# Block 3, recurrent branch: the small products of transitions and outputs grouped by shape, by turns in both column halves

## The chip, the cores and the metric

The kernel runs on one core of one Trainium2 chip. The metric is the device time of one execution in microseconds (us), as the median of several runs. A profile of one execution gives each engine's instructions: PE is the matrix engine's products, PEld its weight loads, DVE the vector engine, ACT the scalar engine, POOL the general one, SP the one that issues most transfers.

## The reference, cut to what matters

The reference chains three transformer blocks over 512 tokens of width 1024. The third block has two mixers side by side: a sparse attention and a recurrence with eight heads of width 64. The recurrence is a scan over the tokens:

```python
def wkv7_scan(r, w, k, v, a, b):
    def step(state, inp):
        r_t, w_t, k_t, v_t, a_t, b_t = inp
        sa = jnp.einsum('bhvk,bhk->bhv', state, a_t)
        state = state * w_t[:, :, None, :] + sa[..., None] * b_t[:, :, None, :] + v_t[..., None] * k_t[:, :, None, :]
        return state, jnp.einsum('bhvk,bhk->bhv', state, r_t)
    ...
    _, ys = lax.scan(step, jnp.zeros((B, H, N, N), jnp.float32), xs)

def rwkv7_mixer(...):
    ...
    y = wkv7_scan(rh, decay.reshape(B, T, H, N), kh, vh, -kk, kk * ah)
    mean = jnp.mean(y, axis=-1, keepdims=True)
    var = jnp.mean(jnp.square(y - mean), axis=-1, keepdims=True)
    y = ((y - mean) * lax.rsqrt(var + GN_EPS)).reshape(B, T, RWKV_WIDTH) * lnx_w + lnx_b
    ...
```

So per token each head's 64 x 64 state is multiplied by a matrix, a rank-one term is added, and the output is the new state times a vector, normalized per head. The mixers' outputs go through a projection and a feed-forward stage.

## The kernel before, in words

The scan is rewritten in 8 chunks of 64 tokens (`CH`, `NCH`), two chunks to a block of 128 tokens. In the function `rwkv_state` the whole is turned into matrix products. Tokens of a chunk or a head's 64 features lie on 64 of the 128 partitions: `half[0]` is partitions 0 to 63, `half[1]` the others. A product `mm(out, w, x)` contracts over the partitions of `w` and `x`; the columns of `w` become the partitions of `out`. So a `w` on 64 partitions uses one half of PE's rows, and an `out` on 64 partitions one half of its columns. The trace writes the shape as rows*columns: 64*64 or 128*64. All operands of these products are fp32, and the trace records each product as two weight loads and two matmuls.

Four small functions do the recurrence:

- `transition(n)` (L2470) makes, for chunk n, the matrix that carries the state over the chunk (`pg`, then added into `GT[:, n]` by DVE) and the chunk's own contribution (`ph`, copied to `S3[:, n]` by ACT). For each of the eight heads it has one product of the shape 64*64 (L2476, not for chunk 0) and one of the shape 128*64 (L2477). Head h writes the column half h % 2.
- `advance(n)` (L2482) multiplies the state into the next one: eight products of the shape 64*64 (L2486), and DVE adds.
- `queries(c)` (L2490) folds a correction into the queries `Rt`: 16 products of the shape 64*64 (L2496) per pair of heads.
- `outputs(tb)` (L2500) makes the outputs of one block of 128 tokens in two halves of four heads (s = 0, 1). For each head and each of the two chunks (e = 0, 1) one product of the shape 64*64 with the state (L2510, not for chunk 0) and one of the shape 128*64 with the chunk's own values (L2511) are added up in PSUM. Chunk e writes column half e. DVE then takes mean and variance per head (L2516, L2517), a reciprocal root (L104 to L108), and normalizes (L2520, L2521).

PSUM tiles come from `k.pst`: four buffers of the tag "g" and two each of "a" and "t". All of `pg`, `ph` and `p` here are "g".

The order of work is set in two places. The code emits in an order of its own: the loop at the end of `rwkv_state` runs transition, advance, queries and outputs with a `yield` after each, and `weave` (L368) runs one step of the attention at each `yield`. An attention step (L2004 on) has four stages of units that lie one step apart: scores on PE (L2093) with maximum on DVE (L2096) and exponential on ACT (L2098), transposes (L2107) with copies (L2108), values (L2117), and the closing of a group (L2120 to L2132). When the recurrence is through, the rest of the attention runs alone. Then a planner in the kernel's framework lays down the order on each engine: it mostly follows the emitted order, but puts an instruction ahead of another whose data or buffer isn't ready by its reckoning.

Of the kernel before, what the change touches and what calls it, by code (L numbers as in the profile page):

```python
# [13 lines left out]
OP = mybir.AluOpType  # L14
# [1712 lines left out]
CH = 64  # L1727
# [618 lines left out]
def rwkv_state(k, pool, dram, a, cst, r, yn):  # L2346

    nc = k.nc
    V, S, G = nc.vector, nc.scalar, nc.gpsimd
    mm = nc.tensor.matmul  # L2350
    BK, UV, GA, eC = r.BK, r.UV, r.GA, r.eC
    half = [slice(0, 64), slice(64, 128)]
    with ExitStack() as ctx:
        def t(shape, name, tag=None, bufs=1, dt=FT):
            return pool.tile(shape, dt, name=k.nm(name), tag=tag or name, bufs=bufs)
# [17 lines left out]
        for s in range(30, -1, -1):  # L2373
            n = 31 - s
# [20 lines left out]
        Rt = pool3.tile([P, 4, T], FT, name="Rt")  # L2395
# [25 lines left out]
        for x in range(32):  # L2421
            for e in range(2):
                mm(pw[x // 16][rows(e, 1), x % 16 * 32:x % 16 * 32 + 32], GAv[rows(e, 0), x, e, 32:64], N1T[rows(e, 0), x],
                   start=True, stop=True)
# [5 lines left out]
        for x in range(32):  # L2430
            for e in range(2):
                mm(pw[x // 16][rows(e, 0), x % 16 * 32:x % 16 * 32 + 32], W[rows(e, 1), x], Nv[rows(e, 1), x, 32:64],
                   start=True, stop=True)
# [10 lines left out]
        Xa = GX[:, 0].rearrange("p (m h d) -> p m h d", m=NT, d=64)  # L2444
        GT = GX[:, 1].rearrange("p (n c d) -> p n c d", n=NCH, d=64)
        G.tensor_tensor(GT, cst["i64"][:, None, None, :].to_broadcast([P, NCH, 4, 64]),
                        eC.rearrange("p c n -> p n c")[:, :, :, None].to_broadcast([P, NCH, 4, 64]), op=OP.mult)
        for m in range(NT):
            F = Fs[m]
            for h0 in (0, 4):  # L2450
# [10 lines left out]
        GR = [t([P, 2, NCH, CH], "GR0", tag="F0"), pool3.tile([P, 2, NCH, CH], FT, name="GR1", tag="F1"),  # L2461
              t([P, 2, NCH, CH], "GR2", tag="N1T"), pool3.tile([P, 2, NCH, CH], FT, name="GR3", tag="W")]
# [5 lines left out]
        S3 = r.zpool.tile([P, NCH, 4, 64], FT, name="S3", tag="zk")  # L2468

        def transition(n):  # L2470
            m, e = divmod(n, 2)
            pg, ph = k.pst("g", (P, 4, 64)), k.pst("g", (P, 4, 64))
            for h in range(8):
                o, hs = half[h % 2], slice(h * 64, (h + 1) * 64)
                if n:
                    mm(pg[o, h // 2], Xa[half[e], m, h], BK[half[e], n, hs], start=True, stop=True)  # L2476
                mm(ph[o, h // 2], BK[:, n, hs], UV[:, m, e, hs], start=True, stop=True)  # L2477
            S.activation(S3[:, n], ph, AF.Copy)
            if n:
                V.tensor_tensor(GT[:, n], GT[:, n], pg, op=OP.add)  # L2480

        def advance(n):  # L2482
            p = k.pst("g", (P, 4, 64))
# [16 lines left out]
        def outputs(tb):  # L2500
            yv = yn[:, tb].rearrange("p (h s d) -> p s h d", s=2, d=64)
            for s in range(2):
                o = slice(s * 64, (s + 1) * 64)
                p = k.pst("g", (P, 4, 64))
                for h in range(s, 8, 2):
                    for e in range(2):
                        n = tb * 2 + e
                        pq = p[half[e], h // 2]
                        if n:
                            mm(pq, Rt[o, h // 2, n * CH:(n + 1) * CH], S3[o, n - 1, h // 2], start=True, stop=False)  # L2510
                        mm(pq, GR[h // 2][:, h % 2, n], UV[:, tb, e, h * 64:(h + 1) * 64], start=n == 0, stop=True)  # L2511
                bs = t([P, 4, 6], "ybs", bufs=2)
                mv = t([P, 4, 2], "ymv", bufs=2)
                rs = t([P, 2, 4], "yrs", bufs=2)
                for h in range(4):
                    V.bn_stats(bs[:, h], p[:, h])  # L2516
                    V.bn_aggr(mv[:, h], bs[:, h])  # L2517
                V.tensor_scalar(rs[:, 0], mv[:, :, 1], 64e-5, None, op0=OP.add)
                k.rsqrt(pool, rs[:, 1], rs[:, 0], 4, [P, 4])
                V.tensor_tensor(yv[:, s], p, mv[:, :, 0:1].to_broadcast([P, 4, 64]), op=OP.subtract)  # L2520
                V.tensor_tensor(yv[:, s], yv[:, s], rs[:, 1][:, :, None].to_broadcast([P, 4, 64]), op=OP.mult)  # L2521

        transition(0)
        for n in range(1, NCH):
            transition(n)
            yield
            if n < NCH - 1:
                advance(n)
            yield
            if n <= 4:  # L2530
                queries(n - 1)
                yield
            if n >= 4:
                outputs(n - 4)
                yield
# [378 lines left out]
```

## Time and profile before

| | |
|---|---|
| median of 3 runs | 3262.9 us (3262.18 to 3266.67) |
| the profiled execution | 3260.15 us |
| its span, first to last instruction | 3258.4 us |
| mean granted clock of PE | 0.966 |
| instructions of the small products, 2702.6 to 2826 us: L2476, L2477 | 112, 128 |
| L2510, L2511 | 112, 128 |

In the rows of groups, the number behind the x is how many instructions there are, then their busy time in us and the mean of one in ns, then the idle time before them. In the rows of the timeline the first number is the start in us, the second the length of that piece; neighbouring pieces of PE overlap, since products are pipelined, so the price of one is read from start to start. In the windows the first columns are the stretch and its length, then each engine's busy time, and then the granted clock of PE as a share of full speed.

### The profile page before, as it was taken

What the parts mean: (1) busy time and instruction counts of PE and PEld (TensorE: products, weight loads), DVE (VectorE), ACT (ScalarE), POOL (GpSimd) and SP (SyncE); (2) the same over time, 40 slices, a digit from 0 to 9 for tenths busy, and PEclk for the clock granted to TensorE, in tenths of its full rate; (3) what the DMA queues carried; (4) which work ended last, traced back from release to release, by engine and by line L of the source; (5) the groups of instructions that cost most, each with busy time, mean ns of one, the idle gap of its engine ahead of it and who ended that gap; (6) DMA issues with size and microseconds to landing.
All of it is one profiled execution on the core that took longest, in us unless ns stands there. A gap on an engine that the chain in (4) does not pass through costs nothing.

```text
span 3258.4 us, 40500 instructions
## 1 busy us (share of the span) xinstructions
PE 3044.4 (93%) x16321; PEld 2319.7 (71%) x16321; DVE 1773.7 (54%) x3227; ACT 1033.1 (32%) x1608; POOL 282.8 (9%) x316
## 2 busy tenths in 40 slices
PE   9899997887787899999999999999999879999999
PEld 7777676443342788888777777888876767688887
DVE  3877755643432544345964656443477775564433
ACT  3666532110010422223323532322223245333221
POOL 0342010000000000001100320000023210000000
PEclk9999998999798999999999999999999989899999
DMA  4322125799899332333223244332333410123322
GB/s 145 97 75 82 62 71 227 317 421 421 354 421 407 108 104 88 107 104 121 94 84 97 87 159 149 104 104 91 104 99 103 137 47 21 66 74 104 100 87 84
DMA packets 240985, 466.38 MB, mean 143 GB/s; under 512 B 24722, under 2 KB 163380, under 8 KB 216732
## 3 DMA queue, kind: packets, MB, share of 16 engines
q1 hardware_dynamic: 230956, 431.95, 36.9%
q0 software_dynamic: 9840, 31.82, 2.9%
q8 instruction: 130, 2.13, 0.3%
q14 instruction: 59, 0.48, 0.0%
HBM read 441.17 MB, written 22.56 MB: 142 GB/s over the span
## 4 chain that ended last, share of the span: by engine, by line
PE 43%; DVE 6%; issue 1%; ACT 1%; POOL 0%; DMA 0%; DVEq 0%; ACTq 0%; POOLq 0%
PE pg L150 20%; PE pg L188 4%; PE pg L189 4%; PE pg L187 4%; DVE nprod L2376 1%; DVE wl L69 1%; PE pg L2117 1%; PE pt L2107 1%; PE pg L176 1%; PE pg L175 1%; PE pg L174 1%; PE pa L2093 1%; PE pt L1442 0%; PE pg L2511 0%; PE pg L2510 0%
## 5 line engine op out<-in xcount | busy, mean ns | idle before, releaser
L69 DVE TENSOR_TENSOR wl<-raw,wh 128x2048 fp32r<-128x2048 f32 (+3 forms) x211 | 438.4, 2078 | 455.9 <-ACT wh L68 455.8
L68 ACT ACTIVATE wh<-raw 128x2048 fp32r<-128x2048 f32 (+3 forms) x214 | 368.8, 1724 | 701.6 <-PE pg L150 344.4
L150 PE MATMUL pg<-x2h,wh 128*128 128x512 f32 (+2 forms) x1136 | 441.9, 389 | 0.0
L150 PE MATMUL pg<-x2h,wl 128*128 128x512 f32 (+2 forms) x1136 | 440.2, 388 | 0.0
L150 PE MATMUL pg<-x2l,wh 128*128 128x512 f32 (+2 forms) x1136 | 439.2, 387 | 0.0
L150 PEld LDWEIGHTS pg<-x2h,wl 128*128 128x128 f32 (+1 forms) x1136 | 212.8, 187 | 49.0 <-issue 7.3
L150 PEld LDWEIGHTS pg<-x2l,wh 128*128 128x128 f32 (+1 forms) x1136 | 212.8, 187 | 47.7 <-issue 6.4
L150 PEld LDWEIGHTS pg<-x2h,wh 128*128 128x128 f32 (+1 forms) x1136 | 212.9, 187 | 45.6 <-issue 3.0
L188 PE MATMUL pg<-wl,hh 128*128 128x512 f32 x608 | 238.5, 392 | 0.0
L189 PE MATMUL pg<-wh,hl 128*128 128x512 f32 x608 | 237.7, 391 | 0.0
L187 PE MATMUL pg<-wh,hh 128*128 128x512 f32 x608 | 236.5, 390 | 0.0
L1178 PE MATMUL pa<-w,mscr 128*32 128x512 f32 x1024 | 172.4, 675 | 51.7 <-DMA w<-w 49.5
L1178 PEld LDWEIGHTS pa<-w,mscr 128*32 128x32 f32 x1024 | 43.3, 122 | 156.8 <-issue 145.0
L188 PEld LDWEIGHTS pg<-wl,hh 128*128 128x128 f32 x608 | 114.2, 188 | 25.4 <-DVE wl L69 0.8
L187 PEld LDWEIGHTS pg<-wh,hh 128*128 128x128 f32 x608 | 114.1, 188 | 25.3
L189 PEld LDWEIGHTS pg<-wh,hl 128*128 128x128 f32 x608 | 114.2, 188 | 23.7
L187 PE MATMUL pg<-wh,x2h 128*128 128x512 f32 (+1 forms) x288 | 101.8, 354 | 2.2 <-ACT x2h L232 2.2
L189 PE MATMUL pg<-wh,x2l 128*128 128x512 f32 (+1 forms) x288 | 101.2, 351 | 0.0
L188 PE MATMUL pg<-wl,x2h 128*128 128x512 f32 (+1 forms) x288 | 100.8, 350 | 0.0
L150 PE MATMUL pg<-x1h,wh 128*128 128x512 f32 x224 | 89.8, 401 | 1.0 <-ACT po L2774 0.6
L150 PE MATMUL pg<-x1l,wh 128*128 128x512 f32 x224 | 89.3, 399 | 0.0
L150 PE MATMUL pg<-x1h,wl 128*128 128x512 f32 x224 | 89.1, 400 | 0.0
(897 smaller groups left out, 5924.6 us busy)
## 6 DMA issues: line engine op xcount, KB each, us to landing
w<-w SPq DMA_DIRECT2D x188, 1024.0 KB
raw<-w_in SPq DMA_DIRECT2D x45, 1024.0 KB
raw<-ffn_w_in SPq DMA_DIRECT2D x44, 1024.0 KB
raw<-w_ff SPq DMA_DIRECT2D x16, 1024.0 KB
raw<-w_ff SPq DMA_DIRECT2D x20, 768.0 KB
raw<-w_in SPq DMA_DIRECT2D x24, 512.0 KB
raw<-w_out SPq DMA_DIRECT2D x12, 1024.0 KB
raw<-ffn_w_out SPq DMA_DIRECT2D x16, 768.0 KB
```

Of the source, the lines that this page charges most:

```text
L68: nc.scalar.activation(h, t, AF.Copy)
L69: (nc.gpsimd if i in self.slow else nc.vector).tensor_tensor(l, t, f32v(h), op=OP.subtract)
L150: nc.tensor.matmul(p, w[:, c, s], x[:, c, t], start=first, stop=last)
L174: nc.tensor.matmul(p[:, t], wh[:, c, s], xh[:, c, t], start=c == 0, stop=False)
L175: nc.tensor.matmul(p[:, t], wh[:, c, s], xl[:, c, t], start=False, stop=False)
L176: nc.tensor.matmul(p[:, t], wl[:, c, s], xh[:, c, t], start=False, stop=c == nk - 1)
L187: nc.tensor.matmul(p, xh[:, c, t], wh[:, c, :ncol], start=start and c == 0, stop=False)
L188: nc.tensor.matmul(p, xh[:, c, t], wl[:, c, :ncol], start=False, stop=False)
L189: nc.tensor.matmul(p, xl[:, c, t], wh[:, c, :ncol], start=False, stop=stop and c == nk - 1)
L1178: nc.tensor.matmul(ph[s], xt[:, c, s], w[:, :, c], start=c == 0, stop=c == DC - 1)
L2093: mm(ps[s], qT[:, c + 4 * s, i * P:(i + 1) * P], kT[:, s, j, :W], start=j == 0, stop=j == 1)
L2107: nc.tensor.transpose(pt[:, j], prs[s][:, j * P:(j + 1) * P], k.ident)
```

## The change

In `transition` the eight products of the first shape come first, then DVE's add into `GT`, then the eight products of the second shape. In `outputs` the eight products of the shape 128*64 come first, by turns in both column halves, and then those of the shape 64*64, by turns as well (for block 0 only half 1 has any). The flag that starts an accumulation is now set once per tile and half, on head pair c = 0, and the later heads' first products find their part of the tile not yet written. The number of products, their operands and all else are the same.

```diff
             pg, ph = k.pst("g", (P, 4, 64)), k.pst("g", (P, 4, 64))
+            if n:
+                for h in range(8):
+                    mm(pg[half[h % 2], h // 2], Xa[half[e], m, h], BK[half[e], n, h * 64:(h + 1) * 64], start=True, stop=True)
+                V.tensor_tensor(GT[:, n], GT[:, n], pg, op=OP.add)
             for h in range(8):
-                o, hs = half[h % 2], slice(h * 64, (h + 1) * 64)
-                if n:
-                    mm(pg[o, h // 2], Xa[half[e], m, h], BK[half[e], n, hs], start=True, stop=True)
-                mm(ph[o, h // 2], BK[:, n, hs], UV[:, m, e, hs], start=True, stop=True)
+                hs = slice(h * 64, (h + 1) * 64)
+                mm(ph[half[h % 2], h // 2], BK[:, n, hs], UV[:, m, e, hs], start=True, stop=True)
             S.activation(S3[:, n], ph, AF.Copy)
-            if n:
-                V.tensor_tensor(GT[:, n], GT[:, n], pg, op=OP.add)
...
-                for h in range(s, 8, 2):
+                for c in range(4):
                     for e in range(2):
                         n = tb * 2 + e
-                        pq = p[half[e], h // 2]
+                        h = 2 * c + s
+                        mm(p[half[e], c], GR[c][:, s, n], UV[:, tb, e, h * 64:(h + 1) * 64], start=c == 0,
+                           stop=n == 0 and c == 3)
+                for c in range(4):
+                    for e in range(2):
+                        n = tb * 2 + e
                         if n:
-                            mm(pq, Rt[o, h // 2, n * CH:(n + 1) * CH], S3[o, n - 1, h // 2], start=True, stop=False)
-                        mm(pq, GR[h // 2][:, h % 2, n], UV[:, tb, e, h * 64:(h + 1) * 64], start=n == 0, stop=True)
+                            mm(p[half[e], c], Rt[o, c, n * CH:(n + 1) * CH], S3[o, n - 1, c], start=False, stop=c == 3)
```

## The prediction

> **What bounds the kernel now.** I read the page first: span, busy shares, and the chain of work that ended last.
>
> ```profile
> span 3258.4 us, 40500 instructions
> PE 3044.4 (93%) x16321; PEld 2319.7 (71%) x16321; DVE 1773.7 (54%) x3227; ACT 1033.1 (32%) x1608; POOL 282.8 (9%) x316
> PE 43%; DVE 6%; issue 1%; ACT 1%; POOL 0%; DMA 0%; DVEq 0%; ACTq 0%; POOLq 0%
> ```
>
> PE leads everywhere, but a share of the whole says nothing of one stage. So I looked up where the four lines of the edit run: L2476 and L2477 (transitions) and L2510 and L2511 (outputs). They lie between 2702.6 and 2826 us. The groups by line, then the windows, of that stretch and of the one ahead of it:
>
> ```profile
> L2511 PE MATMUL pg<-UV,GR 128*64 128x64 f32 x128 | 19.5, 254 | 0.0
> L2510 PE MATMUL pg<-S,Rt 64*64 64x64 f32 x112 | 18.9, 251 | 0.0
> L2477 PE MATMUL pg<-UV,BK 128*64 128x64 f32 x128 | 16.6, 253 | 0.0
> L2476 PE MATMUL pg<-BK,GX 64*64 64x64 f32 x112 | 15.8, 254 | 0.0
> ```
>
> ```profile
> 2702.60:2756.80 54.20, 54.00 (x534) 41.81 (x531) 25.41 (x86) 24.57 (x73) 3.84 (x3) 0.91 0.01 3
> 2756.80:2826.00 69.20, 68.80 (x524) 50.02 (x522) 32.09 (x202) 18.39 (x57) 2.53 (x2) 0.83 0.09 32
> 2680.60:2702.60 22.00, 22.00 (x212) 16.80 (x212) 12.66 (x43) 17.27 (x51) 1.28 (x1) 1.00 0.26 92
> ```
>
> The columns of the windows are PE, PEld, DVE, ACT and POOL busy, the granted clock, the DMA share and GB/s. PE is busy 122.8 of 123.4 us, DVE only 57.5, ACT 43.0, and DMA is nearly idle. Here PE time is kernel time, and the four lines hold some 71 us of busy time on it (records overlap, so the wall time is less; it is cut out below). An x of 128 is 64 products: each is recorded as two instructions.
>
> How PE spends that time shows in the timeline of the transition of chunk 1, which runs in the order of the code:
>
> ```profile
> 2703.25 0.33 PE L2476 MATMUL pg<-BK,GX 64*64 64x64 f32 x2
> 2703.50 0.33 PE L2477 MATMUL pg<-UV,BK 128*64 128x64 f32 x2
> 2703.76 0.32 PE L2476 MATMUL pg<-BK,GX 64*64 64x64 f32 x2
> ...
> 2707.36 0.44 PE L2093 MATMUL pa<-ksT,qT 128*128 128x128 f32 x2
> ```
>
> One product in the 64*64 shape, one in the 128*64 shape, and so on: 16 products from 2703.25 to 2707.36, 0.257 us each from start to start. The transition of chunk 5 has the same products, but there they did not alternate:
>
> ```profile
> 2762.68 0.68 PE L2476 MATMUL pg<-BK,GX 64*64 64x64 f32 x16
> 2763.29 0.85 PE L2093 MATMUL pa<-kwT,qT 128*128 128x256 f32 x4
> 2763.97 0.27 PE L2107 MATMUL pt<-ident,npr 128*128 128x128 f32 x1
> 2764.17 0.69 PE L2477 MATMUL pg<-UV,BK 128*64 128x64 f32 x16
> 2764.79 0.51 PE L2093 MATMUL pg<-kwT,qT 128*128 128x256 f32 x2
> ```
>
> Eight products of one shape, head by head and so by turns in both halves of the output columns, take 0.61 us (2762.68 to 2763.29), the eight others 0.62 (2764.17 to 2764.79): 0.077 us each. That is the order that the change writes for every transition, so its price stands in this trace.
>
> **The change part by part.** Removed: I cut the timeline into the stretches in which the two shapes alternate, and had their lengths added (first stretch and sum; transitions of chunks 1, 2, 3, 4 and 7 in seven pieces, then outputs of all four blocks in eleven):
>
> ```profile
> 2703.25:2707.36 4.11, 4.11 (x37) 1.00 0.02 4
> sum 23.43, PE 23.43; mean PE 3.35
> ```
>
> ```profile
> 2756.82:2761.18 4.36, 4.36 (x52) 3.22 (x48) 1.20 (x8) 0.98 (x4) 0.00 (x0) 1.00 0.01 4
> sum 30.55, PE 30.55 PEld 22.35 DVE 7.63 ACT 5.49 POOL 1.26; mean PE 2.78 PEld 2.03 DVE 0.69 ACT 0.50 POOL 0.12
> ```
>
> Together 54.0 us. Chunks 5 and 6 are already grouped, and chunk 0 has one shape only; nothing is to be had there.
>
> Put back, at full clock: five transitions of 0.61 + 0.62 make 6.15 us. Outputs: blocks 1 to 3 have two halves s each, with eight L2511 products and eight L2510 products, both by turns: 6 x 1.23 = 7.4 us. Block 0 is special. Its first chunk has no state, so only half e = 1 gets L2510 products, four in a row into the same half: grouped by shape, but without turns.
>
> ```profile
> 2757.03 0.33 PE L2510 MATMUL pg<-S,Rt 64*64 64x64 f32 x2
> 2757.29 0.34 PE L2511 MATMUL pg<-UV,GR 128*64 128x64 f32 x4
> 2757.55 0.33 PE L2510 MATMUL pg<-S,Rt 64*64 64x64 f32 x2
> ```
>
> No row shows four such in a row. They cost between 0.077 (as if by turns) and 0.257 us (as if alternating); I take the middle, 0.17, being near neither: 8 x 0.17 + 2 x 0.62 = 2.6 us. The rows also show two L2511 products, of different halves, in the 0.26 us from 2757.29 to 2757.55 that one alone takes elsewhere: the price hangs on the change of shape, hardly on the product. Total back 16.1 us, so PE is relieved of 37.9 us at full clock.
>
> The clock is the second term. It was halved in four stretches:
>
> ```profile
> 2707.90:2711.30 3.40, 3.40 (x28) 2.95 (x27) 1.63 (x6) 1.87 (x6) 0.00 (x0) 0.50 0.01 2
> 2731.80:2738.60 6.80, 6.80 (x39) 5.49 (x39) 2.90 (x8) 2.06 (x6) 0.00 (x0) 0.50 0.00 0
> 2776.20:2783.00 6.80, 6.80 (x30) 4.67 (x28) 4.36 (x30) 1.71 (x4) 0.00 (x0) 0.50 0.00 0
> 2796.60:2813.70 17.10, 17.10 (x72) 11.96 (x71) 7.01 (x40) 3.73 (x11) 1.26 (x1) 0.50 0.21 75
> ```
>
> ```profile
> 2735.71 1.12 PE L2486 MATMUL pg<-S,GX 64*64 64x64 f32 x16
> 2736.76 0.79 PE L2093 MATMUL pa<-kwT,qT 128*128 128x512 f32 x1
> ...
> 2767.00 0.68 PE L2486 MATMUL pg<-S,GX 64*64 64x64 f32 x16
> 2767.61 0.62 PE L2093 MATMUL pg<-kwT,qT 128*128 128x384 f32 x2
> ```
>
> That is 34.1 of 123.4 us, 28%. The same sixteen instructions take 1.05 us in such a stretch and 0.61 outside, a factor of 1.72. So work of length w at full clock takes w / (0.72 + 0.28/1.72) = w / 0.883 at this share. What the change leaves alone, 123.4 - 54.0 = 69.4 us, is then 61.3 us at full clock, and the stage after the change holds 61.3 + 16.1 = 77.4 us. Three readings follow: no halved clock, 77.4 us, 46.0 saved; the same share, 87.7 us, 35.7 saved; halved throughout, 133.1 us, 9.7 lost. All four halved stretches begin in or right behind alternating products, with PE busy all the time, so I expect fewer; but as many alternating stretches (chunks 2 and 4, blocks 0 and 3) have none behind them. I take a third of the way from the same share to none: 39 saved. [...]
>
> New waits are the third term. With PE shorter, the branch beside this one (attention, L2093 to L2117: scores on PE, maximum on DVE, exponential on ACT, transposes and values on PE) has less cover. Lower bound: zero, since in the stage ahead PE was busy 22.00 of 22.00 us with the same attention steps and only light recurrent products. A gain is excluded: no wait stands on PE that could go. Upper bound: what DVE does to free a PSUM tile of the outputs.
>
> ```profile
> L2516 DVE BATCH_NORM_STATS2 ybs<-pg 128x6 f32<-128x64 f32 x32 | 6.5, 215 | 18.6 <-PE pg L2511 18.6
> L2517 DVE BATCH_NORM_AGGREGATE ymv<-ybs 128x2 f32<-128x6 f32 x30 | 4.4, 165 | 0.0
> L2520 DVE TENSOR_TENSOR yn<-pg,ymv 128x256 f32<-128x256 f32 x7 | 2.9, 417 | 0.0
> ```
>
> Four statistics, four aggregates and one subtraction: 4 x 0.215 + 4 x 0.165 + 0.417 = 1.94 us per half, eight halves 15.5 us, if PE stood still in each. I take 5 us, nearer to zero, because in the second window DVE has 32.1 us of work against about 44 left for PE (69.2, less 20.3 in the outputs and 5.2 in chunk 7's transition).
>
> The add to GT moves ahead of the second eight products; it runs on DVE, frees its PSUM tile 0.62 us sooner, and costs nothing. In the outputs the accumulation starts once per tile and half instead of once per product; the instructions are as many as before. No DMA or queue is touched.
>
> Sum: 39 - 5 = 34 us. The profiled execution took 3260.15 us (1.75 above its span), so 3226 there; the three runs' median, 3262.9, lies 2.75 above it. Forecast **3229 us**.
>
> **The rivals.**
> 1. DVE takes the place of PE: the outputs' statistics end last and the PSUM tiles come free late. For it: outputs crowd into the second window. Against: DVE's 32.1 against 44. It loses another 15.5 of the 39 - 5: 18.5 saved, 3244 us.
> 2. The halved clock goes away altogether: 46.0 - 5 = 41, up to 46 with no new wait: 3217 to 3222 us. For it: where the four stretches begin. Against: the four exceptions.
> 3. The change doesn't do what it says. What runs isn't quite what the code emits (chunk 5 above, with attention products between its groups); the planner could cut the groups up. Each product would again pay up to 0.257: 3263 us.
> 4. Turns in columns don't overlap. The row first: L2486 changes row half and column half at each product and takes 0.61 per eight; L2476 keeps its row half, changes only columns, and takes 0.61 too. So the row half makes no difference, and this rival has that against it; were the price of a column turn 0.257, nothing would be saved: 3263 us. [...]
> 5. Slower: the denser small products keep the clock halved through the whole stage. Price 9.7 us worked out above: 3273 us. It turns to a loss once the halved share passes nine tenths (123.4 = 77.4 / (1 - 0.42 x share)); now it is 28%.
>
> **How the numbers follow.** Forecast 0.74, rival 1 0.12, rival 2 0.08, rival 3 0.03, rival 4 0.01, rival 5 0.02. The range goes from rival 2's ends to rival 1: 3216 to 3245. About 0.2% of the time, 6.5 us, is what a measurement can tell from no change. Forecast and rivals 1 and 2 are beyond that: faster 0.94; rivals 3 and 4 same, 0.04; rival 5 slower, 0.02.
>
> **What would show it.** Right: L2476's and L2477's successors as groups of x16 about 0.6 us apart; the stage from the first transition to the last output below 95 us; fewer rows at clock 0.50; the chain still on PE. The new-wait term is wrong if PE's idle time there is over 10 us, with L2516 or L2520 as releaser. The forecast is wrong if groups appear but spacing stays near 0.26 (rival 4), if they are cut into pairs (rival 3), or if the stage keeps its length at clock 0.50 (rival 5).

## The result, and the profile after

| | before | after |
|---|---|---|
| median of 4 runs each | 3264.78 us (3262.18 to 3267.94) | 3213.80 us (3211.15 to 3215.34) |
| the profiled execution | 3260.15 us | 3213.74 us |
| its span | 3258.4 us | 3212.0 us |

The ratio of after to before is 0.9846, with a 95% interval from 0.9835 to 0.9858: 46 to 54 us saved. The forecast was 34, and the time lies 2 us below the range. The way was right and the size too small.

The page after, the same three lines as before: span, engines, and the chain that ended last.

```profile
span 3212.0 us, 40496 instructions
PE 3000.2 (93%) x16321; PEld 2285.5 (71%) x16321; DVE 1774.1 (55%) x3227; ACT 1034.0 (32%) x1608; POOL 282.7 (9%) x316
PE 42%; DVE 6%; issue 1%; ACT 1%; POOL 0%; DMA 0%; DVEq 0%; ACTq 0%; POOLq 0%
```

PE's busy time fell by 44.2 us with as many instructions; DVE, ACT and POOL stayed within a microsecond. Nothing was moved to another engine.

The timeline after: the transition of chunk 1, and the outputs of block 0 (line numbers are those of the changed file: L2475 and L2479 are the products of the transitions, L2511 and L2517 those of the outputs).

```profile
2703.45 0.68 PE L2475 MATMUL pg<-BK,GX 64*64 64x64 f32 x16
2704.07 0.69 PE L2479 MATMUL pg<-UV,BK 128*64 128x64 f32 x16
2704.68 0.44 PE L2093 MATMUL pa<-ksT,qT 128*128 128x128 f32 x2
...
2741.28 0.63 PE L2511 MATMUL pg<-UV,GR 128*64 128x64 f32 x16
2741.85 0.68 PE L2517 MATMUL pg<-S,Rt 64*64 64x64 f32 x8
2742.45 0.69 PE L2511 MATMUL pg<-UV,GR 128*64 128x64 f32 x16
```

Chunk 1 takes 1.23 us where it took 4.11, as summed. The row at 2741.85 is the one that the prediction could not price: four products in a row into one column half take 0.60 us (to 2742.45), 0.15 each, beside the 0.17 that was assumed.

The whole stage, from the first transition to the last output, in windows before and after (in later windows PE's busy time stands alone):

```profile
2702.69:2824.57 121.88, 121.29 (x1042) 90.66 (x1038) 56.08 (x275) 42.61 (x128) 6.37 (x5) 0.86 0.05 19
```

```profile
2702.89:2778.78 75.89, 75.30 (x1041) 59.53 (x1037) 55.99 (x272) 42.70 (x128) 6.40 (x5) 1.00 0.08 31
```

It is 46.0 us shorter, and that is all but 0.4 us of what the span lost. Two columns tell the story: the clock went from 0.86 to 1.00, with no halved stretch left, and PE is idle for 0.59 us, as little as before. The lengths of the grouped products, added up as in the prediction, first of the transitions (chunks 1 to 4 and 7) and then of the outputs, give what was put back (the first stretch and the sum of each):

```profile
2703.45:2704.68 1.23, 1.23 (x36) 1.00 0.07 20
sum 6.62, PE 6.62; mean PE 0.95
```

```profile
2741.28:2743.67 2.39, 2.39 (x52) 1.00 0.03 7
sum 11.03, PE 11.03; mean PE 1.00
```

So 54.0 us became 17.65 (16.1 was forecast, at full clock): 36.3 of the 46.0. The other work of the stage went from 67.9 to 58.2 us with the same instructions. Of the 34.1 us that ran at half clock before, 21.8 lay in this other work; at the factor of 1.72 that is worth 9.1 of the 9.7 us.

### The profile page after: what moved, and what is told of

Read it like the earlier page. It is cut to its first block, busy times and chain, and to the rows that moved or that the text cites. A ratio compares the mean times of both kernels' runs of the same rounds, so it can differ in the third digit from the quotient of the medians.

```text
span 3212.0 us, 40496 instructions
## 1 busy us (share of the span) xinstructions
PE 3000.2 (93%) x16321; PEld 2285.5 (71%) x16321; DVE 1774.1 (55%) x3227; ACT 1034.0 (32%) x1608; POOL 282.7 (9%) x316
## 4 chain that ended last, share of the span: by engine, by line
PE 42%; DVE 6%; issue 1%; ACT 1%; POOL 0%; DMA 0%; DVEq 0%; ACTq 0%; POOLq 0%
PE pg L150 20%; PE pg L188 4%; PE pg L189 4%; PE pg L187 4%; DVE wl L69 1%; DVE nprod L2376 1%; PE pg L175 1%; PE pg L176 1%; PE pg L174 1%; PE pg L2117 1%; PE pt L2107 1%; PE pa L2093 0%; PE pt L1442 0%; PE pg L1691 0%; DVE Ninv L2378 0%
```

## The experiments

The theory after the result: a change of shape is what costs, and a run of such changes also brings the halved clock, which then slows everything behind it. The rivals: the cost lies in the column halves; or the gain comes from one of the two functions; or the clock would have recovered anyway. Each of the first five kernels was compared with runs of the kernel before on the same chip (medians 3262.05 us for the first four, 3260.13 for the fifth), so their ratios are compared rather than their times. The last five kernels have one run each. The changed kernel was not run again beside them, and the kernel before took some 4 us less there than beside the changed kernel (3260.13 and 3260.66 against 3264.78). Their differences from the changed kernel, 3213.80 us, are good to a few microseconds only; the readings rest on their traces.

**Transitions alone, and outputs alone.** The first keeps the old `outputs`, the second the old `transition`.

> Only the transitions are grouped; the outputs are as before. By the sum (23.4 us of alternating transitions replaced by 6.2) it saves 17 us of PE time: about 3248 us where the kernel before takes 3265. If alternating products also bring on the halved clock, chunks 1, 3 and 7 lose their halved stretches and another 2 to 6 us go: 3242 to 3246, while the outputs keep theirs. If the gain came from anywhere else than these products, it stays at 3265.

> Only the outputs are grouped; the transitions are as before. By the sum it saves 30.5 - 10.0 = 20.5 us of PE time: about 3244 us; with halved stretches of blocks 1 and 2 gone too, 3238 to 3243. If clock and products are two separate terms, the savings of this kernel and of the one with transitions alone add up to the 51 us of the whole change within 6 us; if the halved clock needs both kinds to be gone, they add up to clearly less than 45.

Transitions alone: 3249.24 us, ratio 0.9957 (0.9941 to 0.9974), 14 us saved. Outputs alone: 3235.22 us, ratio 0.9918 (0.9901 to 0.9934), 27 us saved. The sum is 41 of the 50 us that the ratio of the whole change stands for. Each part is known to some 5 us and the whole to 4, so the 9 us that are missing are hardly more than the noise, and that the two parts depend on each other is suggested by them, not shown. The windows of the first kernel, over the stretches of its outputs at half clock, point the same way:

```profile
2748.10:2758.30 10.20, 10.20 (x68) 0.50 0.00 1
2768.50:2771.90 3.40, 3.40 (x14) 0.51 0.00 0
2785.60:2799.30 13.70, 13.70 (x76) 0.50 0.19 69
2806.10:2819.70 13.60, 13.60 (x63) 0.50 0.00 1
```

With the outputs still alternating, 41 us of the stage ran at half clock, against 34.1 before, although the transitions had become short. (This is one execution, of 3253.58 us, the longest of the four.) The expectation that chunks 1, 3 and 7 would take halved stretches with them failed: two went, and the outputs got more. With the outputs grouped, only two stretches were left, right at chunks 1 and 3:

```profile
2707.40:2710.80 3.40, 3.40 (x28) 0.50 0.01 2
2731.30:2738.10 6.80, 6.80 (x37) 0.50 0.00 0
```

**Shape without turns, and turns without shape.** The first groups by shape, but writes one column half four times and then the other. The second keeps the shapes alternating and, in the outputs of blocks 1 to 3, changes the column half at every product. In the transitions it doesn't do that, though its expectation says so: there it only swaps the heads of a pair, and the halves run 0, 1, 1, 0, so that one is still written twice running, as before. The test lies in the outputs.

```diff
-                for h in range(8):
+                for h in (0, 2, 4, 6, 1, 3, 5, 7):
                     mm(pg[half[h % 2], h // 2], ...)
...
-                for c in range(4):
-                    for e in range(2):
+                for e in range(2):
+                    for c in range(4):
```

```diff
                 mm(pg[o, h // 2], Xa[half[e], m, h], BK[half[e], n, hs], start=True, stop=True)
-                mm(ph[o, h // 2], BK[:, n, hs], UV[:, m, e, hs], start=True, stop=True)
+                g = h ^ 1
+                gs = slice(g * 64, (g + 1) * 64)
+                mm(ph[half[g % 2], g // 2], BK[:, n, gs], UV[:, m, e, gs], start=True, stop=True)
...
+                    for c in range(4):
+                        st(c, 0, c == 0, False)
+                        gr(c, 1, c == 0, False)
+                    for c in range(4):
+                        gr(c, 0, False, c == 3)
+                        st(c, 1, False, c == 3)
```

(`st` is the product with the state, `gr` the other; for block 0, which lacks one of the four kinds, the orders are similar.)

> Grouped by shape, but within a group first the four products of one column half and then the four of the other. If a change of shape is what costs, a product without turns costs what the four in a row of block 0 cost in the changed kernel (0.60 us for four, 0.15 each) against 0.077 with turns: 232 such products x 0.073 = 17 us more than the changed kernel, 3231 us. If writing the same column half twice running is what costs, nearly every product pays 0.257: 3255 to 3265 us.

> The shapes alternate at every product as before (in blocks 1 to 3 and in all transitions), but now the column half changes at every product too. If a change of shape is what costs, nothing is gained: 3258 to 3268 us and 0.257 us from start to start. If the same column half twice running is what costs, most of the gain of the whole change is here: 3214 to 3222 us.

Without turns: 3223.78 us, ratio 0.9882 (0.9865 to 0.9898), so 38.5 of the 50 us remain. Turns alone: 3263.03 us, ratio 1.0001 (0.9991 to 1.0011): nothing. The timelines of the two, a transition of the first and outputs of block 1 of the second:

```profile
2703.07 0.96 PE L2475 MATMUL pg<-BK,GX 64*64 64x64 f32 x16
2703.97 0.97 PE L2479 MATMUL pg<-UV,BK 128*64 128x64 f32 x16
```

```profile
2774.36 0.33 PE L2509 MATMUL pg<-S,Rt 64*64 64x64 f32 x2
2774.62 0.33 PE L2507 MATMUL pg<-UV,GR 128*64 128x64 f32 x2
2774.88 0.33 PE L2509 MATMUL pg<-S,Rt 64*64 64x64 f32 x2
```

The change of shape is what costs: alternating products stay at 0.26 us each whatever their columns. Turns are worth something only within a shape: a group of eight takes 0.90 us without them and 0.61 with them. The stage has 29 such groups of eight; 29 x 0.29 = 8.4 us, near the 9.5 by which the span is longer (3221.5 against 3212.0). The expected 17 us was too much: it took the 0.15 each of four in a row for all, but a group of eight still changes its half once and changes its shape once for all eight.

**Pairs.** Two products of one shape, one to each column half, then two of the other.

```diff
+            for c in range(4):
+                for h in (2 * c, 2 * c + 1):
+                    if n:
+                        mm(pg[half[h % 2], c], ...)
+                for h in (2 * c, 2 * c + 1):
+                    mm(ph[half[h % 2], c], ...)
```

> Two products of one shape (both column halves), then two of the other, and so on: half as many changes of shape as before. If each change of shape costs and the second product of a pair is nearly free, a pair takes 0.26 us and the 54 us of alternating products become about 27: 27 us saved, and with part of the halved clock gone up to 33: 3232 to 3238 us. If the cost lay in columns, it would be as quick as the changed kernel, 3214.

3229.20 us, ratio 0.9903 (0.9883 to 0.9922): 31.6 us saved, within what was expected by shape. Its timeline:

```profile
2703.25 0.33 PE L2476 MATMUL pg<-BK,GX 64*64 64x64 f32 x4
2703.51 0.34 PE L2479 MATMUL pg<-UV,BK 128*64 128x64 f32 x4
2703.77 0.33 PE L2476 MATMUL pg<-BK,GX 64*64 64x64 f32 x4
```

Two products in the 0.26 us that one took: the second of a pair is free. The stage kept one halved stretch, of 6.8 us, right behind the outputs of block 0 (4.11 us, 2744.60 to 2748.71). There the order by pairs changes nothing: block 0 already had two products of one shape and one of the other in the kernel before, and the shape still changes every 0.26 us.

**Bursts: is it the alternation that halves the clock?** Extra products into a tile that nobody reads, ahead of the advance of chunk 2; all else as in the changed kernel. The first burst alternates 128 products, the second has 416 in two groups.

```diff
+            if n == 2:
+                q = k.pst("g", (P, 4, 64))
+                for i in range(8):
+                    for h in range(8):
+                        hs = slice(h * 64, (h + 1) * 64)
+                        mm(q[half[h % 2], h // 2], Xa[half[0], 1, h], BK[half[0], 2, hs], start=True, stop=True)
+                        mm(q[half[h % 2], h // 2], BK[:, 2, hs], UV[:, 1, 0, hs], start=True, stop=True)
```

> The changed kernel with 128 extra products ahead of the advance of chunk 2, whose shapes alternate, into a PSUM tile that nobody reads; the outputs are the same. If alternating products bring on the halved clock, it falls to 0.50 within 4 to 8 us of the burst's start and stays there: 128 x 0.257 = 33 us at full clock, 45 to 52 us with the clock halved (0.40 each), so 3259 to 3268 us. If they do not, the clock stays at 1.00 and it costs 33 us: 3247.

> The changed kernel with 416 extra products at the same place, 208 of one shape by turns and then 208 of the other: 416 x 0.077 = 32 us, as long as the alternating burst at full clock. If it is the alternation that brings on the halved clock, the clock stays at 1.00 here: 3246 us. If small products as such do it, the clock falls here too and the burst takes 50 us or more: 3264.

The alternating burst cost 50 us (3263.73 against 3213.8), the grouped one 25 us (3238.89) for more than three times the products. The windows over the first burst and behind it, and then those of the second:

```profile
2715.75:2721.50 5.75, 5.75 (x47) 1.00 0.00 0
2721.50:2764.09 42.59, 42.59 (x212) 0.50 0.00 1
2764.09:2769.30 5.21, 5.21 (x61) 0.50 0.00 0
2769.30:2775.00 5.70, 5.70 (x84) 1.00 0.01 3
```

```profile
2716.63:2741.19 24.56, 24.56 (x834) 1.00 0.02 4
2741.19:2790.00 48.81, 48.22 (x662) 1.00 0.01 2
```

PE is busy all the time in both. Alternating, the clock falls 5.75 us after the start, stays at 0.50 to the end and for another 5.2 us; grouped, it stays at 1.00 through 24.6 us. So here it is the alternation, not small products as such, that brings the halved clock. What about the alternation does it isn't separated: the two bursts differ in the changes of shape and also in how little PE gets done, one product in 0.257 us against one in 0.059. A burst of one shape, with pauses that long between its products, was not run. The grouped burst was also cheaper than expected: 24.56 / 416 = 0.059 us a product instead of 0.077. A group of eight at 0.61 us is thus 8 x 0.059 and 0.14 us for the change of shape.

**Short and long bursts.** The same 60 alternating products in six bursts of ten, or in two of thirty (`n < 7` and `range(5)`, or `n in (2, 5)` and `range(15)`, in the loop above).

> The changed kernel with 60 extra alternating products in six bursts of ten, one ahead of the advance (or its place) of each of chunks 1 to 6, into a tile that nobody reads; outputs the same. The halved stretches seen so far are multiples of 3.4 us, and their ends lie on one grid of 3.41 us. If the clock falls only after a grid interval that is nearly filled with alternating products (in the kernel before: those filled to 84% and more, none of those filled to 82% and less), a burst of 2.6 us can fill at most 75% and the clock stays at 1.00 in this stage: 60 x 0.257 = 15.4 us, 3229 us. If the amount of alternating work in the stage counts, some intervals at 0.50 appear and it takes 3232 us or more.

> The same 60 products in two bursts of 30, ahead of the advances of chunks 2 and 5. A burst of 7.7 us always holds a whole grid interval, so by the interval theory the clock falls to 0.50 in or right after each of the two for 3.4 to 10 us: 15.4 us and 1.4 to 4 us more for each, 3232 to 3237 us. If the amount counts, this kernel and the one with six short bursts take the same time within 1 us and have the same halved share.

Six short bursts: 3230.53 us, 16.7 more than the changed kernel, clock 1.00 all through:

```profile
2702.00:2782.00 80.00, 79.80 (x1038) 1.00 0.03 9
```

Two long ones: 3233.60 us, 19.8 more, with 6.8 us at half clock for each:

```profile
2716.44:2721.90 5.46, 5.46 (x45) 1.00 0.00 0
2721.90:2728.70 6.80, 6.80 (x45) 0.50 0.01 2
2728.70:2758.00 29.30, 29.11 (x409) 1.00 0.01 2
2758.54:2766.27 7.73, 7.73 (x66) 1.00 0.00 0
2766.27:2773.10 6.83, 6.83 (x52) 0.50 0.01 2
```

The 3.1 us between the two kernels say little, with one run each; the clock does: the same 60 products brought the halved clock in long runs and not in short ones, so their amount doesn't decide. Length isn't all either. In the kernel before, the transition of chunk 4 is as long a run as that of chunk 1 (4.11 us), and no halved stretch follows it:

```profile
2743.75:2747.86 4.11, 4.11 (x34) 1.00 0.01 4
```

What the trace shows to differ is where the run lies on a grid of 3.41 us intervals (the four halved stretches of the kernel before end at 2711.30, 2738.60, 2783.00 and 2813.70 us, so 8, 13 and 9 times 3.41 us apart): chunk 1 fills 85% of the interval ahead of its halved stretch, chunk 4 at most 71% of one. But the border of the expectation, between 82 and 84%, doesn't hold in the other traces: in the kernel with the outputs alone grouped, an interval filled to 78% (2703.96 to 2707.37) is followed by a halved one, while in the kernel before one filled to 83% (2769.32 to 2772.74) is not. What else counts stays open.

**Twice the statistics: how much DVE had to spare.**

```diff
-                for h in range(4):
-                    V.bn_stats(bs[:, h], p[:, h])
-                    V.bn_aggr(mv[:, h], bs[:, h])
+                for h in range(8):
+                    V.bn_stats(bs[:, h % 4], p[:, h % 4])
+                    V.bn_aggr(mv[:, h % 4], bs[:, h % 4])
```

> The changed kernel with the statistics and aggregates of every output half made twice (the second time over the first; outputs the same): 32 x (0.215 + 0.165) = 12.2 us more on DVE. The outputs' part of the stage has 37.5 us with 30.9 us of DVE work now. If DVE had 6.6 us to spare and PE waits for the rest, the time rises by about 5 us, and PE shows idle time released by DVE. If the waits that the prediction put at 5 us were already there in another form, each microsecond more on DVE shows fully: 12 us. If DVE's tail is hidden behind the attention's end too, nothing is seen: below 2 us.

3220.13 us: 6.3 more. The rows of the statistics and aggregates grew by 10.7 us, DVE's busy time over the whole execution by 5.2 (from 1774.1 to 1779.3). PE's waits in the stage and its tail now name DVE's reciprocal root:

```profile
PE pg L2479 <- DVE yrs L104: 2.3, 2, 1.8
...
PE pt L2128 <- DVE yrs L108: 0.8, 1, 0.8
...
PE pt L2107 <- DVE yrs L108: 0.6, 1, 0.6
```

So the bound by DVE is real. The clock shows there too, over the interval with the 1.8 us wait and the next:

```profile
2745.78:2749.19 3.41, 1.66 (x37) 1.00 0.00 0
2749.19:2752.60 3.41, 3.41 (x17) 0.50 0.00 0
```

The stage itself grew by 4.8 us: 2.9 of them are waits for DVE (the 2.3 and the 0.6 above), and the halved interval costs about 1.4 by the factor of 1.72, an estimate. How much more work DVE could take without PE waiting isn't settled by one kernel.

## Why the prediction was right in kind and too small

The mechanism of the products was right: PE's time was the kernel's time, the alternation cost 0.257 us a product, the form of chunk 5 was the price of the new order, and the planner kept the groups, with only some attention products between them. The step that failed is the size of two other terms of the sum, the clock above all, and the rest lies between executions:

- *The clock*, "I take a third of the way from the same share to none: 39 saved". It went to none, and the stage saved 46.0. The burst experiments show why the third was wrong: the clock was halved for 42.59 us of the alternating burst and not at all in the 24.56 us of the grouped one, so with the alternation all of it went. The exceptions that the prediction counted against this (chunks 2 and 4, blocks 0 and 3) don't speak against that: of two runs of 4.11 us one was followed by the halved clock and the other not, and they lie differently on the 3.41 us grid (85% of an interval for chunk 1, 71% for chunk 4, above). 7 us.
- *New waits*, "I take 5 us". There were none: PE is idle for 0.59 us of the stage, before and after. The stage ahead, full at 22.00 of 22.00, was the right row to go by. (By the prediction's own rows the 20.3 us that it takes off for the outputs is 20.5; nothing hangs on it.) 5 us.
- Outside the stage the span lost 0.4 us. The other 4.6 us are between executions: the sum was made against a profiled execution of 3260.15 us, and the median of before in this comparison is 3264.78; other sets of runs of it gave 3262.05 and 3260.13. The forecast had added 2.75 us because the median of before lay that far above the profiled execution; after the change the two agree (3213.80 and 3213.74).

7 + 5 + 0.4 + 4.6 make the 17 us between 34 and 51. The term of the products was nearly right: 17.65 us put back where 16.1 was summed, since the planner let attention products split some of the groups.

That the stage saved 46.0 us, to the decimal what the reading without a halved clock gave, is luck. Two errors of 1.5 us cancel: the products put back 1.55 us more, and the other work took 59.8 us where 61.3 was summed (58.2, and 1.5 behind the last output that the prediction's window holds). It had been at half clock for 32% of its time, not for the 28% of the whole stage that the sum applied to it, and that is most of the difference.

Of the rivals, the second came true (no halved clock, no new wait). Its chance of 0.08 was low for what the trace already showed, four halved stretches that all begin in or right behind alternating products, and the range ended with it, where the spread of the runs of before should have been added. DVE did not take over, though doubled statistics make PE wait 2.9 us for it in the stage. Rival 4 is refuted by the group of eight: 0.61 us with turns in columns alone, 0.90 without. Rival 5 had the sign of the clock term wrong: the dense small products of the changed stage ran at 1.00, and so did 416 of them in a burst of 24.56 us.

With doubled statistics the clock fell behind an interval with 1.66 us of work in 3.41. In the alternating burst it fell behind 5.75 us in which the trace has PE busy for 5.75, and in the grouped one it stayed at 1.00 with PE busy for 24.56 of 24.56 us. PE's recorded busy time alone does not tell what the clock will do.

## What to carry to other kernels

Look along PE's timeline for neighbours whose shape (rows*columns) differs from one product to the next; put those of one shape together, and by turns in both column halves within the group (here 0.077 us a product in groups of eight, where alternating ones took 0.257). Price the change from a place in the same trace where a group already stands, and read the granted clock beside it: if halved stretches begin in the work to be removed, count the slowness of what lies behind them as part of the gain.

## What the runs showed of the hardware that was not expected

- In a burst of alternating shapes PE's clock was halved though PE is recorded as busy without a gap: 42.59 us at 0.50, and none in 24.56 us of grouped products.
- Ten alternating products at a time (2.6 us) did not bring the halved clock in any of six bursts, thirty (7.7 us) did both times, for 6.8 us each; sixteen (4.11 us) did for chunk 1 of the kernel before and not for chunk 4.
- A change of shape costs 0.14 us for a group of eight (0.61 - 8 x 0.059) and 0.20 us where every product changes (0.257 - 0.059), at full clock; at half clock an alternating product takes 0.40.
- In the one execution traced, grouping the transitions alone left the stage with more time at half clock than before (41 us against 34.1); grouping the outputs alone left 10.2.
